# Stage transitions, LN3's residual and the mixer's constants placed elsewhere in a decoder layer on one core

## The chip, the cores and the metric

The kernel runs on one core of a Trainium2 chip. The core has a tensor engine (TensorE, PE in the profile; its weight loads are PEld), a vector engine (DVE), a scalar engine (ACT), GpSimd (POOL) and a sync engine (SP). They run their own instruction streams in order and wait for each other on semaphores. DMAs are issued from the queues of SP, ACT and POOL. The metric is the device time of one execution in microseconds (us); lower is better.

## The reference

One hybrid decoder layer on 256 tokens of width 2048, all in float32:

```
h = LN1(ALPHA*x + 0.5 * SwiGLU(x; ffn1))          # D_FF = 5632
m = mixer(h)      # latent attention (8 heads, RoPE) and differential attention (4 heads, ALiBi),
                  # both projected to 2048, gated by sigmoids, summed, times w_out
h = LN2(ALPHA*h + m)
out = LN3(ALPHA*h + 0.5 * SwiGLU(h; ffn2))

SwiGLU(x) = (silu(x @ w_gate) * (x @ w_up)) @ w_down
LN(x)     = (x - mean) * rsqrt(var + 1e-5) * g + b
```

ALPHA is 2 to the 1/4. The differential attention needs a causal mask with a slope times the distance of positions; RoPE needs sines and cosines of angles made from the positions; a scalar lambda is made from four small vectors.

## The kernel before

**Units.** Every product with a large weight matrix goes through one pipeline of *units* (`unit`, `advance`). A unit loads two 128-row blocks of weights, 512 columns wide (512 KB), splits them into a high part (cast to float32r on ACT, line 192) and a remainder (subtraction on DVE, line 193), and multiplies. Each product is the sum of three (high by high, low by high, high by low), so a unit has six 128x512 matmuls for each half `b` of the tokens (line 255). The split pairs live in a ring of `wring` tiles. Loads run a few units ahead, splits a few units ahead of the matmuls (`look(3, 4)` usually, `look(3, 2)` with the wide ring).

**Sevens.** Most matrix work is done in groups of seven products where eight would be needed: sums of weight blocks and of activations are formed first. Some of these sums are made by DVE (line 352), some by a DMA on POOL's queue that accumulates into a loaded block (line 357). Other units are *plain*: one load on SP's queue, one split, twelve matmuls. Results are read from PSUM with snapshots on ACT (line 428) and additions on DVE.

**Ticks.** The program's order is written by hand. `later(n, fn)` writes `fn` into the program n units on; `plan.at(i, fn)` attaches it to unit i; with `True` it is written when the unit is created. `tick()` ends every unit. Below this, the compiler's planner places each engine's instructions: by priority, which is the written order unless it is raised, among those that its own estimate of time says are ready. Once placed, each engine's order is fixed.

**Held-back halves.** Around a LayerNorm the second half of each unit (b=1) is held back: `widen()` sets `lag[0] = LAG` (seven units) and a ring of ten pairs, so that the b=0 products of the last units come first; `catch_up(n)` writes held halves until n remain. `one_lag` ends this.

**LayerNorm.** `LayerNorm.__init__` fetches the residual in four 128x1024 tiles `z` over POOL's queue and prepares it: for LN1 a multiplication by ALPHA on ACT; for LN2 and LN3, whose input `res` was stored before gain and shift were applied, a DVE multiplication and a DVE addition a tile with rows `gb` (line 523), themselves scaled by ALPHA on ACT (line 514). `evac` adds a finished PSUM bank to `z` (549 or 551) and takes statistics (553), all under a raised priority of 300 instructions. At the last chunk it calls `apply`, still under that priority: variance, square root, four normalised chunks (580), and at once the transposes `rows_to_quad` (458) with their copies into the next stage's activations, and a store of each chunk to `res`. LN3 has no transposes; its gain and shift rows come from `take_rows`, four loads at once, at the last eight units of the down pass.

**The feed-forward part** (`ffn`): gate/up units (opening of 16, then ten groups of 22), then the down pass in two column passes (`i` = 0 and 1) of sevens and plain (`lone`) units. The LayerNorm object is made at the first down unit.

**Around the mixer.** `setup` (mask on POOL, five small loads) is attached before the last eight units of FFN1's second down pass; `constants` follows 18 ticks later, that is in the mixer's opening: biases (769), angles and their range reduction (775 to 788), lambda (791 to 799). The opening ends with `kr_done`, whose transposes (816) feed the rotary key. `qr_finish` and the branch's `done1` transpose their rows two and four ticks after the last product.

Of the kernel before, what the change touches and what calls it, by code (L numbers as in the profile page):

```python
# [11 lines left out]
F32 = mybir.dt.float32  # L12
# [3 lines left out]
ALU = mybir.AluOpType  # L16
AX = mybir.AxisListType

P = 128
# [3 lines left out]
KD = D // P  # L23
# [9 lines left out]
LAG = 7  # L33
# [28 lines left out]
def layer_kernel(ctx: ExitStack, tc: tile.TileContext, a: dict, out: bass.AP):  # L62
# [15 lines left out]
    def act_tile(shape, dt=F32, name="act"):  # L78
        return apool.tile(shape, dt, tag="act", name=nm(name), bufs=SLOTS)
# [39 lines left out]
    class Acts:  # L119
        def __init__(self, name, kept=()):  # L120
            self.name = name
            self.kept = kept
            self.tiles = {}
            self.ready = set()
            self.raws = {}
            self.forms = {}
# [360 lines left out]
        V.scalar_tensor_tensor(out=f, in0=t, scalar=3.0, in1=y, op0=ALU.add, op1=ALU.mult)  # L487
        return f

    def broadcast_rows(src):  # L490
        r = []
        for h in range(2):
            t = act_tile([P, 1024], F32, "gb")
            nc.gpsimd.dma_start(t, src[0:1, h * 1024:(h + 1) * 1024].partition_broadcast(P))
            r.append(t)
        return r

    class LayerNorm:
        def __init__(self, scale, residual, last, each, x=None, cols=None, prior=None):
            self.scale = scale  # L500
            self.x = x
            self.cols = None
            if cols is not None:
                self.cols = [small.tile([P, KD], F32, tag="cols", name=nm("cols"), bufs=4) for _ in range(2)]
                for t, src in zip(self.cols, cols):
                    nc.gpsimd.dma_start(t, src)
            self.each = each
            self.z = [[None, None], [None, None]]
            rows = {}

            def row(i, h):
                t = rows[i, h] = act_tile([P, 1024], F32, "gb")
                nc.gpsimd.dma_start(t, prior[i][0:1, h * 1024:(h + 1) * 1024].partition_broadcast(P))
                later(6, lambda: S.mul(t, t, ALPHA))

            def fetch(b, h):
                t = self.z[b][h] = act_tile([P, 1024], F32, "z")
                nc.gpsimd.dma_start(t, residual[b, :, h * 1024:(h + 1) * 1024])
                if prior is None:
                    later(8, lambda: S.mul(t, t, ALPHA))  # L520
                else:
                    for i, op in ((0, ALU.mult), (1, ALU.add)):
                        later(7 + i, lambda i=i, op=op: V.tensor_tensor(out=t, in0=t, in1=rows[i, h], op=op))  # L523
            n = 0
            for h in range(2):
                jobs = [] if prior is None else [lambda i=i, h=h: row(i, h) for i in range(2)]
                for f in jobs + [lambda b=b, h=h: fetch(b, h) for b in range(2)]:
                    later(n, f)
                    n += 2
            self.rows = last  # L530
            self.gb = None
            self.stats = [small.tile([P, 4, 6], F32, tag="bn", name=nm("bn"), bufs=4) for _ in range(2)]

        def take_rows(self):
            if self.cols is None:
                self.gb = [broadcast_rows(r) for r in self.rows]

        def at(self, c, b):
            return self.z[b][c // 2][:, (c % 2) * 512:(c % 2) * 512 + 512]
# [5 lines left out]
        def evac(self, c, b, bank):  # L545
            z = self.at(c, b)
            with tc.high_priority(offset=PRIOR):
                if self.scale == 1.0:
                    V.tensor_tensor(out=z, in0=bank, in1=z, op=ALU.add)
                else:  # L550
                    V.scalar_tensor_tensor(out=z, in0=bank, scalar=self.scale, in1=z,
                                           op0=ALU.mult, op1=ALU.add)
                V.bn_stats(self.stats[b][:, c, :], z)  # L553
                if c == 2 and b == 0:
                    S.activation(sm(1, "sq"), self.stats[b][:, c, 0:1], AF.Sqrt, scale=0.0)
                if c == 3:
                    self.apply(b)

        def apply(self, b):
            mv = sm(2, "mv")  # L560
            V.bn_aggr(mv, self.stats[b].rearrange("p a s -> p (a s)"))
            zs = [self.at(c, b) for c in range(4)]

            if self.cols is None:
                gs, bs = ([self.gb[i][c // 2][:, (c % 2) * 512:(c % 2) * 512 + 512] for c in range(4)] for i in range(2))

                def center(c):
                    V.scalar_tensor_tensor(out=zs[c], in0=zs[c], scalar=mv[:, 0:1], in1=gs[c],  # L568
                                           op0=ALU.subtract, op1=ALU.mult)
                r = rstd(mv[:, 1:2], LN_EPS, 1, lambda: center(0))  # L570
                for c in range(4):
                    if c > 0:
                        center(c)
                    V.scalar_tensor_tensor(out=zs[c], in0=zs[c], scalar=r, in1=bs[c],
                                           op0=ALU.mult, op1=ALU.add)
                    self.each(b, c, zs[c])
                return
            r = rstd(mv[:, 1:2], LN_EPS, 1)
            for c in range(4):
                V.tensor_scalar(out=zs[c], in0=zs[c], scalar1=mv[:, 0:1], scalar2=r,  # L580
                                op0=ALU.subtract, op1=ALU.mult)
                rows_to_quad(zs[c], b, self.x, c, *self.cols)
                self.each(b, c, zs[c])

    def ffn(n, x, wgu, wdn, residual, rows, each, first=None, nxt=None, cols=None, prior=None):
        hb = {}
# [35 lines left out]
            (ahead_of if first is not None else at)(i + 10, f)  # L622
        if first is not None:
            first(at, ahead_of)
        at(16, one_lag)

        hx = [Acts("h") for _ in range(2)]
# [13 lines left out]
        for i, (c0, c1) in enumerate(((0, 1), (2, 3))):  # L641
# [62 lines left out]
                return [lambda k=k: step(k) for k in range(5)]  # L704

            if i == 0:
                at(len(items), lambda: st.update(ln=LayerNorm(0.5, residual, rows, each, nxt, cols, prior)), True)
            items += lone(4)
            items += seven(0, (5, 6), False)
            items += lone(7)  # L710
            if i == 0:
                items += seven(1, (8, 9), True)
                items += lone(10)
            else:
                items += seven(1, (8,), True)
                if n == 1:
                    at(len(items), setup)
                at(len(items), lambda: st["ln"].take_rows(), True)
                at(len(items), widen, True)
                for m in range(2):  # L720
                    for q in (9, 10):
                        items += lone(q, (m, m), True)
# [19 lines left out]
    def setup():  # L742
        GP.memset(mask, 0.0)
        for o in (0, 256):
            GP.affine_select(out=mask[:, o:o + P], in_=mask[:, o:o + P], pattern=[[-1, P]],
                             compare_op=ALU.is_ge, fill=NEG, base=0, channel_multiplier=1)
        pos_i = sm(2, "pos_i", I32)
        nc.gpsimd.dma_start(pos_i, a["pos_col"])
        row_i = tmp_tile([P, T], "row_i", I32)
        nc.gpsimd.dma_start(row_i, a["pos_row"].partition_broadcast(P))  # L750
        invf = tmp_tile([P, HALF], "invf")
        nc.gpsimd.dma_start(invf, a["inv_freq"].partition_broadcast(P))
        lv = tmp_tile([P, 4, P], "lv")
        nc.gpsimd.dma_start(lv.rearrange("p a n -> p (a n)"), a["lam"].partition_broadcast(P))
        nc.gpsimd.dma_start(subg, a["subln_g"].partition_broadcast(P))
        later(18, lambda: constants(pos_i, row_i, invf, lv))

    def constants(pos_i, row_i, invf, lv):
        pos = sm(2, "pos")
        V.tensor_copy(pos, pos_i)  # L760
        npos = sm(2, "npos")
# [6 lines left out]
        for h in range(DH):  # L768
            V.scalar_tensor_tensor(out=bias[h], in0=dist, scalar=-SLOPES[h], in1=mask,
                                   op0=ALU.mult, op1=ALU.add)  # L770

        ang = tmp_tile([P, 2, 2, HALF], "ang")
        for b in range(2):
            for j in range(2):
# [12 lines left out]
        V.tensor_scalar(out=ang, in0=ang, scalar1=PI_LO, scalar2=-PI_LO, op0=ALU.min, op1=ALU.max)  # L787
        S.activation(sincos, ang, AF.Sin)

        lp = tmp_tile([P, 2, P], "lp")  # L790
        V.tensor_tensor(out=lp, in0=lv[:, 0:2, :], in1=lv[:, 2:4, :], op=ALU.mult)
        ls = sm(2, "ls")
# [52 lines left out]
    def mixer(x, norm):  # L845
# [96 lines left out]
        def qr_finish(n, b, bank):  # L942
            t = tmp_tile([P, 512], "qr")
            tv = t.rearrange("p (h j i) -> p h j i", h=MH, j=2)
            rope(tv[:, :, 0, :], tv[:, :, 1, :], bank, b, MH)
            later(2, lambda: park_cols(t, qrp[b]))

        items += opening(x, [a[f"wc{n}"][0] for n in range(3)], c_done, (512, 288, 288))
        for i, f in enumerate(x.sevens(0)):
# [146 lines left out]
        def branch(f):  # L1096
# [5 lines left out]
            def done1(b, bank):  # L1102
                V.tensor_tensor(out=g1[:, b, :], in0=bank, in1=g1[:, b, :], op=ALU.mult)
                V.tensor_tensor(out=g0[:, b, :], in0=g0[:, b, :], in1=g1[:, b, :], op=ALU.add)
                later(4, lambda: rows_to_quad(g0[:, b, :], b, yq, f))

            def open_gates():
                for t in (g0, g1):
# [122 lines left out]
```

## Time and profile before

| | us |
|---|---|
| median of 3 runs | 2042.49 |
| lowest, highest | 2042.34, 2049.31 |
| the profiled execution | 2040.43 |
| its span, first to last instruction | 2038.4 |

The profile is of one execution. Its page gives busy time by engine, the span in slices, DMA queues and the costliest groups; further views answer for a stretch of time or a line: groups of instructions, an engine's timeline with the idle time before each piece and what ended it, waits between engines, and busy time and granted TensorE clock by window. Times in them are us from the start of the span. By the timeline FFN1's gate/up runs to about 452, its down pass to about 711, the mixer to about 1318 with w_out last, FFN2's gate/up to about 1775, and its down pass to 2027; LN3 ends the program.

### The profile page before, as it was taken

What the parts mean: (1) busy time and instruction counts of PE and PEld (TensorE: products, weight loads), DVE (VectorE), ACT (ScalarE), POOL (GpSimd) and SP (SyncE); (2) the same over time, 40 slices, a digit from 0 to 9 for tenths busy, and PEclk for the clock granted to TensorE, in tenths of its full rate; (3) what the DMA queues carried; (4) which work ended last, traced back from release to release, by engine and by line L of the source; (5) the groups of instructions that cost most, each with busy time, mean ns of one, the idle gap of its engine ahead of it and who ended that gap; (6) DMA issues with size and microseconds to landing.
All of it is one profiled execution on the core that took longest, in us unless ns stands there. A gap on an engine that the chain in (4) does not pass through costs nothing. (4 is left out here: it accounts for less than half of the span.)

```text
span 2038.4 us, 25557 instructions
## 1 busy us (share of the span) xinstructions
PE 1986.5 (97%) x8908; PEld 1636.8 (80%) x8908; DVE 1679.2 (82%) x1955; ACT 1250.0 (61%) x1587; POOL 280.0 (14%) x429
## 2 busy tenths in 40 slices
PE   9999999999999999999999999999999999989997
PEld 8888888877888778888878788778888888768885
DVE  7888888888989887588888675568888888899897
ACT  6666666666656686566667644466666666656563
POOL 1211121111000000211111100002111211110010
PEclk9999999999999999999999999999999999999999
DMA  9888888898879677898887955568888888898784
GB/s 317 232 252 250 247 231 251 245 289 272 277 254 271 201 222 247 227 287 249 263 254 229 340 198 192 173 232 247 249 245 240 242 244 252 280 296 274 249 265 157
DMA packets 160129, 506.64 MB, mean 249 GB/s; under 512 B 18992, under 2 KB 28288, under 8 KB 160000
## 3 DMA queue, kind: packets, MB, share of 16 engines
q1 hardware_dynamic: 99072, 352.89, 49.2%
q0 software_dynamic: 35104, 115.94, 25.9%
q10 hardware_dynamic: 25824, 36.18, 5.3%
q8 instruction: 69, 1.13, 0.2%
q14 instruction: 60, 0.49, 0.1%
HBM read 474.01 MB, written 30.93 MB: 248 GB/s over the span
## 5 line engine op out<-in xcount | busy, mean ns | idle before, releaser
L255 PE MATMUL mm<-wring,h 128*128 128x512 f32 (+1 forms) x3456 | 800.8, 386 | 11.3 <-DVE h L193 5.2
L255 PEld LDWEIGHTS mm<-wring,h 128*128 128x128 f32 x3456 | 635.5, 188 | 148.3 <-DVE h L193 8.4
L192 ACT CAST wring<-sraw 128x1024 fp32r<-128x1024 f32 x490 | 510.7, 1051 | 387.0 <-DVE sraw L352 123.5
L255 PE MATMUL mm<-wring,xs 128*128 128x512 f32 x2940 | 704.2, 391 | 5.9 <-ACT wring L192 4.4
L193 DVE TENSOR_TENSOR wring<-sraw,wring 128x1024 fp32r<-128x1024 f32 x490 | 592.5, 1218 | 121.0 <-ACT wring L192 113.7
L193 DVE TENSOR_TENSOR wring<-raw,wring 128x1024 fp32r<-128x1024 f32 (+1 forms) x462 | 548.9, 1204 | 166.9 <-ACT wring L192 165.2
L255 PEld LDWEIGHTS mm<-wring,xs 128*128 128x128 f32 x2940 | 551.4, 188 | 123.1 <-ACT wring L192 5.7
L192 ACT CAST wring<-raw 128x1024 fp32r<-128x1024 f32 (+1 forms) x462 | 471.2, 1040 | 284.9 <-PE mm L255 167.9
L255 PE MATMUL mm<-wring,x 128*128 128x512 f32 x1152 | 269.3, 390 | 1.9 <-ACT snap L428 1.8
L255 PEld LDWEIGHTS mm<-wring,x 128*128 128x128 f32 x1152 | 215.7, 188 | 48.6 <-ACT snap L428 2.8
L352 DVE TENSOR_TENSOR sraw<-sraw,sraw 128x1024 f32<-128x1024 f32 x140 | 168.6, 1218 | 0.3
L357 POOL DMA_DIRECT2D sraw<-in_gu_dram x80 | 69.4, 872 | 477.3 <-DMA raw<-in_gu_dram 295.4
L593 POOL DMA_DIRECT2D hT<-blocks x176 | 97.3, 562 | 205.9 <-DVE blocks L591 204.1
L255 PE MATMUL mm<-wring,y 128*128 128x512 f32 x384 | 89.1, 390 | 0.0
L255 PEld LDWEIGHTS mm<-wring,y 128*128 128x128 f32 x384 | 72.2, 188 | 14.9
L357 POOL DMA_DIRECT2D sraw<-in_dn_dram x32 | 27.3, 853 | 391.1 <-DVE wring L193 245.5
L428 ACT COPY snap<-mm 128x512 f32<-128x512 f32 x108 | 62.4, 578 | 5.0 <-PE mm L255 5.0
L612 DVE TENSOR_TENSOR gus<-mm,snap 128x512 f32<-128x512 f32 x80 | 54.8, 685 | 3.9 <-PE mm L255 3.9
L599 ACT ACTIVATE sg<-gus 128x256 f32<-128x256 f32 x80 | 33.2, 415 | 24.6 <-DVE gus L612 24.6
L255 PE MATMUL mm<-wring,om 128*128 128x512 f32 x192 | 46.0, 397 | 0.0
L255 PE MATMUL mm<-wring,od 128*128 128x512 f32 x192 | 44.2, 389 | 0.0
L255 PEld LDWEIGHTS mm<-wring,om 128*128 128x128 f32 x192 | 36.6, 192 | 7.6
(233 smaller groups left out, 1003.4 us busy)
## 6 DMA issues: line engine op xcount, KB each, us to landing
raw<-in_gu_dram SPq DMA_DIRECT2D x192, 512.0 KB, 4.7
sraw<-in_gu_dram SPq DMA_DIRECT2D x120, 512.0 KB, 6.9
raw<-in_dn_dram SPq DMA_DIRECT2D x112, 512.0 KB, 5.2
sraw<-in_gu_dram POOLq DMA_DIRECT2D x80, 512.0 KB, 8.0
sraw<-in_dn_dram SPq DMA_DIRECT2D x48, 512.0 KB, 6.9
hraw<-hT ACTq DMA_DIRECT2D x44, 512.0 KB, 5.0
sraw<-in_dn_dram POOLq DMA_DIRECT2D x32, 512.0 KB, 8.8
raw<-in_w_out_dram SPq DMA_DIRECT2D x32, 512.0 KB, 3.3
```

What stands on the lines that cost most here:

```text
L192: S.copy(hi, src)
L193: V.tensor_tensor(out=lo, in0=src, in1=hi.bitcast(F32), op=ALU.subtract)
L255: PE.matmul(o, x, w, start=first and i == 0, stop=last and i == len(whole) - 1, skip_group_check=True)
L352: V.tensor_tensor(out=t, in0=t, in1=self.blocks[joins[p], s], op=ALU.add)
L357: nc.gpsimd.dma_start(self.blocks[adds[p], s], self.w[1][4 * d + s], accum_op=ALU.add)
L428: S.copy(st["t"][i], bk[n])
L593: nc.gpsimd.dma_start(hT[q, b].rearrange("(g r) (i f) -> i r g f", g=4, i=4)[i], t[32 * i:32 * (i + 1), :].rearrange("r (g f) -> r g f", g=4))
L599: S.activation(sg, gate, AF.Silu)
L612: V.tensor_tensor(out=t, in0=bank, in1=snap, op=op)
```

## The change

1. `LayerNorm.apply` is divided. `normalise` (statistics, chunks, stores) keeps the raised priority. The transposes go to `turn`, outside it. For b=0 it writes four held halves, the transposes of chunk 0, one half, chunk 1, one half, chunk 2, one half, chunk 3, and sets the lag to zero, so that the last unit's b=1 half follows at once. For b=1 it writes chunk c's transposes 4 + c ticks later and sets the lag to seven again for the next stage.
2. For LN3 the residual's gain, shift and ALPHA are applied in FFN2's gate/up, from unit 46 on: `polish` fetches rows and tiles five ticks apart, multiplies, adds, and stores the result back to `res`. LN3's object then only fetches it, two ticks apart. LN2's fetches come three ticks apart instead of two.
3. LN3's gain and shift rows are loaded one a unit, attached to the last eight units' first four, instead of four at once when the first of them is created.
4. `setup` moves to the end of FFN1's first down pass, and `constants` is divided into masks, angles and lambdas, 6, 7 and 8 ticks after it, in plain units.
5. The transposes of `qr` come three ticks after their product instead of two, those of the branch's rows five instead of four.

```diff
+    def halves(residual, prior, gap, got, done=None, raw=False):
+        rows = {}
+        def row(i, h):
+            t = rows[i, h] = act_tile([P, 1024], F32, "gb")
+            nc.gpsimd.dma_start(t, prior[i][0:1, h * 1024:(h + 1) * 1024].partition_broadcast(P))
+            later(6, lambda: S.mul(t, t, ALPHA))
+        def fetch(b, h):
+            t = act_tile([P, 1024], F32, "z")
+            nc.gpsimd.dma_start(t, residual[b, :, h * 1024:(h + 1) * 1024])
+            got(b, h, t)
+            if raw:
+                later(8, lambda: S.mul(t, t, ALPHA))
+            if prior is None:
+                return
+            for i, op in ((0, ALU.mult), (1, ALU.add)):
+                later(7 + i, lambda i=i, op=op: V.tensor_tensor(out=t, in0=t, in1=rows[i, h], op=op))
+            if done is not None:
+                later(9, lambda: done(b, h, t))
+        n = 0
         for h in range(2):
...
+            for f in jobs + [lambda b=b, h=h: fetch(b, h) for b in range(2)]:
+                later(n, f)
+                n += gap
+    def polish(res, prior):
+        def back(b, h, t):
+            nc.gpsimd.dma_start(res[b, :, h * 1024:(h + 1) * 1024], t)
+        halves(res, prior, 5, lambda b, h, t: None, back)
...
+            halves(residual, prior, 2 if prior is None else 3, got, raw=raw)
...
-        def take_rows(self):
-            if self.cols is None:
-                self.gb = [broadcast_rows(r) for r in self.rows]
+        def take_row(self, i, h):
+            if self.gb is None:
+                self.gb = [[None, None], [None, None]]
+            t = self.gb[i][h] = act_tile([P, 1024], F32, "gb")
+            nc.gpsimd.dma_start(t, self.rows[i][0:1, h * 1024:(h + 1) * 1024].partition_broadcast(P))
...
                 if c == 3:
-                    self.apply(b)
-        def apply(self, b):
+                    self.normalise(b)
+            if c == 3 and self.cols is not None:
+                self.turn(b)
+        def normalise(self, b):
...
-                rows_to_quad(zs[c], b, self.x, c, *self.cols)
                 self.each(b, c, zs[c])
+        def turn(self, b):
+            def one(c):
+                rows_to_quad(self.at(c, b), b, self.x, c, *self.cols)
+            if b == 0:
+                for c in range(4):
+                    catch_up(3 - c)
+                    one(c)
+                lag[0] = 0
+            else:
+                for c in range(4):
+                    later(4 + c, lambda c=c: one(c))
+                lag[0] = LAG
...
+        if prior is not None:
+            at(KD + 30, lambda: polish(residual, prior))
...
-                at(len(items), lambda: st.update(ln=LayerNorm(0.5, residual, rows, each, nxt, cols, prior)), True)
+                at(len(items), lambda: st.update(ln=LayerNorm(0.5, residual, rows, each, nxt, cols, None, prior is None)), True)
...
                 items += seven(1, (8, 9), True)
+                if n == 1:
+                    at(len(items) - 4, setup)
                 items += lone(10)
             else:
                 items += seven(1, (8,), True)
-                if n == 1:
-                    at(len(items), setup)
-                at(len(items), lambda: st["ln"].take_rows(), True)
+                if rows is not None:
+                    for k in range(4):
+                        at(len(items) + k, lambda k=k: st["ln"].take_row(k % 2, k // 2))
                 at(len(items), widen, True)
...
-        later(18, lambda: constants(pos_i, row_i, invf, lv))
+        for k, part in enumerate(constants(pos_i, row_i, invf, lv)):
+            later(6 + k, part)
     def constants(pos_i, row_i, invf, lv):
+        return [lambda: masks(pos_i, row_i), lambda: angles(pos_i, invf), lambda: lambdas(lv)]
...
-            later(2, lambda: park_cols(t, qrp[b]))
+            later(3, lambda: park_cols(t, qrp[b]))
...
-                later(4, lambda: rows_to_quad(g0[:, b, :], b, yq, f))
+                later(5, lambda: rows_to_quad(g0[:, b, :], b, yq, f))
```

More of the change, by code (lines that the diff above doesn't have):

```diff
@@ L488, in rstd, with __init__ @@
         return f
-    def broadcast_rows(src):
-        r = []
-        for h in range(2):
[L493 to L496, printed above, removed]
+    def halves(residual, prior, gap, got, done=None, raw=False):
[17 more added lines that the diff above has]
+        n = 0
+        for h in range(2):
+            jobs = [] if prior is None else [lambda i=i, h=h: row(i, h) for i in range(2)]
+            for f in jobs + [lambda b=b, h=h: fetch(b, h) for b in range(2)]:
[5 more added lines that the diff above has]
+        halves(res, prior, 5, lambda b, h, t: None, back)
     class LayerNorm:
-        def __init__(self, scale, residual, last, each, x=None, cols=None, prior=None):
+        def __init__(self, scale, residual, last, each, x=None, cols=None, prior=None, raw=False):
             self.scale = scale
@@ L508, in __init__, with got @@
             self.z = [[None, None], [None, None]]
[L509 to L529, printed above, removed]
+            def got(b, h, t):
+                self.z[b][h] = t
+            halves(residual, prior, 2 if prior is None else 3, got, raw=raw)
             self.rows = last
@@ L755, in setup, with masks @@
         nc.gpsimd.dma_start(subg, a["subln_g"].partition_broadcast(P))
-        later(18, lambda: constants(pos_i, row_i, invf, lv))
+        for k, part in enumerate(constants(pos_i, row_i, invf, lv)):
+            later(6 + k, part)
     def constants(pos_i, row_i, invf, lv):
+        return [lambda: masks(pos_i, row_i), lambda: angles(pos_i, invf), lambda: lambdas(lv)]
+    def masks(pos_i, row_i):
         pos = sm(2, "pos")
@@ L770, in constants, with angles @@
                                    op0=ALU.mult, op1=ALU.add)
+    def angles(pos_i, invf):
+        pos = sm(2, "pos")
+        V.tensor_copy(pos, pos_i)
         ang = tmp_tile([P, 2, 2, HALF], "ang")
@@ L788, in constants, with lambdas @@
         S.activation(sincos, ang, AF.Sin)
+    def lambdas(lv):
         lp = tmp_tile([P, 2, P], "lp")
```

## The prediction

> **What bounds the kernel now.** The first part of the page shows TensorE busy nearly throughout, so I asked the windows view what an undisturbed stretch looks like.
>
> ```profile
> span 2038.4 us, 25557 instructions
> PE 1986.5 (97%) x8908; PEld 1636.8 (80%) x8908; DVE 1679.2 (82%) x1955; ACT 1250.0 (61%) x1587; POOL 280.0 (14%) x429
> 200.00:300.00 100.00, 100.00 (x443) 82.66 (x442) 85.26 (x89) 62.20 (x75) 17.47 (x26) 1.00 0.85 244
> ```
>
> The window row gives us, then busy time of PE, PEld, DVE, ACT and POOL, granted clock, DMA share and GB/s. 443 matmuls fill 100 us, so one takes 0.226 us, a half unit of six 1.36 us, a whole unit 2.71 us. No matmul is added or removed: the change can only win back the time in which TensorE stands still, and the half clock that follows. So I read the idle times in the PE timeline, stage by stage (in brackets: idle before, and what ended it).
>
> ```profile
> 692.72 1.94 PE L458 MATMUL tr<-ident,z 128*128 128x128 f32 x16 [1.81 <-DVE z L580]
> 694.41 16.62 PE L255 MATMUL mm<-wring,h 128*128 128x512 f32 x86
> 712.12 2.02 PE L458 MATMUL tr<-ident,z 128*128 128x128 f32 x16 [1.09 <-DVE z L580]
> 715.23 1.22 PE L255 MATMUL mm<-wring,h 128*128 128x512 f32 x3 [1.09 <-ACT h L192]
> 762.02 0.30 PE L816 MATMUL tr<-ident,kr_row 128*128 128x128 f32 x1 [2.90 <-DVE kr_row L811]
> 827.91 0.63 PE L888 MATMUL tr<-ident,qr 128*128 128x128 f32 x4 [1.35 <-DVE qr L811]
> 1167.45 0.66 PE L458 MATMUL tr<-ident,rows 128*128 128x128 f32 x4 [1.43 <-DVE rows L1104]
> 1169.78 1.12 PE L458 MATMUL tr<-ident,rows 128*128 128x128 f32 x4 [1.68 <-DVE rows L1104]
> 1312.41 3.45 PE L458 MATMUL tr<-ident,z 128*128 128x128 f32 x16 [4.60 <-DVE z L580]
> 1315.51 1.89 PE L255 MATMUL mm<-wring,y 128*128 128x512 f32 x6
> 1340.95 2.02 PE L458 MATMUL tr<-ident,z 128*128 128x128 f32 x16 [0.43 <-DVE z L580]
> 1344.06 2.15 PE L255 MATMUL mm<-wring,h 128*128 128x512 f32 x7 [1.09 <-ACT h L192]
> ```
>
> In each the tensor engine has reached a transpose whose rows DVE hasn't finished. In the LN2 transition (1312) old matmuls (y) still run after the transposes: work was there to cover the 4.60 us.
>
> **LayerNorm transposes and held-back halves.** The change puts four held halves, 24 matmuls, 5.4 us, between the last b=0 half and the first transpose, and a half ahead of each later chunk. LN2: 5.4 covers 4.60; the idle time goes. The sixteen transposes there took 3.45 instead of 1.94, at half clock:
>
> ```profile
> 1312.40:1315.90 3.50, 3.49 (x17) 3.50 (x18) 1.61 (x4) 2.53 (x7) 2.35 (x4) 0.53 0.56 199
> ```
>
> so 1.51 go with it. For b=1 the transposes come four ticks later, behind three units of the next stage, 18 matmuls as before: 0.43 stays. The next stage's b=1 halves now wait up to seven units, so the 1.09 for ACT's h goes. LN2: 4.60 + 1.51 + 1.09 = **7.2** (bounds: 1.1, the last part alone, and 7.6, with the 0.43). At LN1 much of the cover exists already:
>
> ```profile
> 688.36 0.68 DVE L551 SCALAR_TENSOR_TENSOR z<-mm,z 128x512 f32<-128x512 f32 x1
> 692.02 1.92 DVE L580 TENSOR_SCALAR z<-z,mv,f 128x512 f32<-128x512 f32 x4
> ```
>
> PE ran until 690.91, past the start of the b=0 evacuation at 688.36, so held halves already stood there. I take 0.5 of the 1.81, keep the first 1.09, drop the second: **1.6** (0 to 4.0). The transposes lose their priority, and with them the copies and splits behind them on ACT and DVE; the next stage's first unit comes four halves and three groups of transposes after the first, at least 5.4 us, against about 3.1 between transposes and h in the second pair of rows (712.12 to 715.23): hidden; uncovered it costs the 1.09 again.
>
> **Later transposes.** qr comes one whole unit later, 2.71 against 1.35: **1.35** (0 to 1.35). The branch's rows likewise: 1.43 + 1.68 = 3.11, less 2.71: **2.7** (0 to 3.11). For the last branch this leaves one unit less before w_out reads y: the copies need under the 2.71 that remain, so 0; if a ring cast gets ahead on ACT, 1.1. LN2's residual loads go out every third unit instead of every second, on POOL: this only thins a burst, I count 0.
>
> **Masks and angles.** They leave the mixer's opening, where kr waits:
>
> ```profile
> L785 DVE SCALAR_TENSOR_TENSOR ang<-turns,ang 128x128 f32<-128x128 f32 x12 | 3.4, 286 | 0.0
> L769 DVE SCALAR_TENSOR_TENSOR bias<-dist,mask 128x384 f32<-128x384 f32 x4 | 2.0, 551 | 0.0
> L472 ACT ACT_TABLE_LOAD x2 | 2.6, 1283 | 0.0
> L795 ACT ACT_TABLE_LOAD x1 | 1.3, 1283 | 0.0
> L788 ACT ACT_TABLE_LOAD x1 | 1.3, 1283 | 0.0
> 755.00:767.00 12.00, 8.95 (x37) 6.72 (x36) 9.18 (x19) 9.75 (x16) 0.00 (x0) 0.86 0.58 159
> 1160.00:1172.00 12.00, 8.89 (x39) 7.00 (x38) 9.86 (x12) 7.52 (x9) 0.00 (x0) 0.89 0.79 295
> ```
>
> With the other small operations they are some 9 us of DVE (5.4 in these two rows; the rest an estimate from that), and the square root then needs no table load of 1.28 in the opening, since neither sine nor exponential is called in between. Of 2.90 I take about half, **1.5** (0 to 2.9): the second kr row still waits on ACT copies that queue behind ring casts. The clock means of 0.86 and 0.89 over 12 us stand for 1.7 and 1.3 us at most; with shorter waits I take **1.0** of these (0 to 3.0).
>
> The Trainium skill, in "TensorE: Matmul & The Clock Gate", section "What's actually happening", has the clock halved after a whole idle window of about 3.4 us. The row speaks against it in that strict form: 2.90 us idle sufficed. By the rule the 1.0 would be nothing and the sum 1.0 less.
>
> In plain down units the 9 us land on a stretch whose DVE is full:
>
> ```profile
> 564.00:572.00 8.00, 8.00 (x37) 6.60 (x37) 7.35 (x9) 6.54 (x9) 0.00 (x0) 1.00 0.92 327
> 572.00:580.00 8.00, 8.00 (x37) 6.63 (x36) 8.00 (x14) 3.32 (x4) 0.00 (x0) 1.00 0.67 243
> 596.00:604.00 8.00, 8.00 (x37) 6.64 (x36) 4.70 (x5) 4.62 (x5) 0.00 (x0) 1.00 0.93 303
> ```
>
> Cover: four prepared units, up to 10.8 us where all are plain; the deficit is worked off after 596. Cost: **2** of 0 to 9, near the lower end because of the cover. The five small loads and POOL's mask are moved ahead of the second pass's accumulating DMAs on POOL; POOL is idle in the first two of these rows, so nothing. No load of SP's queue is moved.
>
> **LN3's residual.** FFN2's down pass loses eight DVE and four ACT operations and four row loads. Its twin in FFN1 never had the DVE part:
>
> ```profile
> 1774.00:1831.00 57.00, 47.96 (x206) 38.27 (x206) 51.55 (x57) 36.63 (x48) 10.04 (x16) 1.00 0.89 292
> 452.00:509.00 57.00, 54.99 (x239) 44.14 (x238) 50.67 (x58) 40.33 (x52) 7.90 (x12) 1.00 0.87 283
> L523 DVE TENSOR_TENSOR z<-z,gb 128x1024 f32<-128x1024 f32 x8 | 9.8, 1219 | 0.0
> L514 ACT ACTIVATE gb<-gb 128x1024 f32<-128x1024 f32 x4 | 4.2, 1059 | 4.2 <-DMA gb<-in_ln_g_dram 3.8 <-DMA gb<-in_ln_b_dram 0.4
> ```
>
> PE idles 9.04 of 57 us there and 2.01 in the twin. **7.0** (4 to 9: 9 is all of the idle time, 4 the ACT time that goes if DVE's share turns out to have been waiting time anyway; the twin, which I take, says what stays late, since it keeps all other work of the stage). In gate/up the same work returns, with four stores and a second set of loads, spread over 44 units:
>
> ```profile
> 1418.00:1500.00 82.00, 81.84 (x362) 67.44 (x360) 70.55 (x73) 50.88 (x61) 15.78 (x24) 1.00 0.84 244
> DVE z L523 <- DMA z<-res: 5.7, 1, 5.7
> z<-res POOLq DMA_DIRECT2D x8, 512.0 KB, 13.0
> sraw<-in_gu_dram POOLq DMA_DIRECT2D x80, 512.0 KB, 8.0
> GB/s 317 232 252 250 247 231 251 245 289 272 277 254 271 201 222 247 227 287 249 263 254 229 340 198 192 173 232 247 249 245 240 242 244 252 280 296 274 249 265 157
> ```
>
> DVE's free time, 11.45 of 82 us, holds the 9.8, leaving 1.7: nearly saturated, but four units of lead cover a burst. DMA carries 12 x 0.52 MB more, 77 GB/s beside 244; the 321 together are under the 340 that one slice of the page reaches, so I count no DMA bound. POOL's queue takes twelve issues; behind a store that waits for DVE stand the accumulating DMAs of the sevens, and behind these the casts on ACT that read them. ACT's four multiplications can hold up the snapshots behind them, as the 4.2 us of waiting for row loads above show for the down pass. Cost: **2** of 0 to 9.8, because the free time is there on paper and only its lumps are not.
>
> **End of the down pass.** LN3's gain and shift rows are loaded one a unit, no longer four at once:
>
> ```profile
> 1995.68 4.74 PE L255 MATMUL mm<-wring,xs 128*128 128x512 f32 x18 [1.51 <-ACT wring L192]
> 1983.71 10.08 DMA raw<-in_dn_dram
> ```
>
> A raw load took 10.08 us behind them. They are still 2 MB in the same stretch: **0.5** of 0 to 1.5; landing too late for LN3 would cost about 1.
>
> **Sum.** 7.2 + 1.6 + 1.35 + 2.7 + 1.5 + 1.0 + 7.0 + 0.5 = 22.85, less 4 = 18.85 us. The profiled execution took 2040.43 (span 2038.4), so 2021.6; against the median of 2042.49, which lies 2.1 higher, 2023.6. All gains at their upper and costs at their lower ends give 2009, all the other way 2058.
>
> **Rivals.**
> 1. *DVE becomes the bound* in gate/up and the plain units: both costs at their ends, 9.8 + 9 instead of 4, 14.8 more: 2038.4. For it: 8.00 of 8.00 at 572, 98% forecast at 1418. Against: PE never stopped at 572.
> 2. *The order on TensorE isn't the written one.* Instructions are placed by a planner's estimate; if it brings the transposes forward again, LN1 and LN2 keep their waits, 8.8 more: 2032.4. Against: the transposes lose the priority that had put them ahead of the y matmuls.
> 3. *Slower: POOL's queue in gate/up.* A store or load that waits in order holds the accumulating DMAs behind it, eight in 82 us, and a later seven needs each (landing 8.0 already). The one wait measured for such a residual is 5.7; eight times that is 45.6, less one cover of 7.4 (four units at 82/44 us): 38 lost, 2062. It decides from (18.85 + 7.4 + 10.2) / 8 = 4.6 us each. Against: the spacing of five units thins the burst in which 5.7 arose.
>
> **Chances.** 0.5% of the median, about what a measurement of this kernel can tell from no change, is 10.2 us: faster below 2032.3, slower above 2052.7. Forecast 0.62 (its own range 2011 to 2032), rival 1 0.16 (same), rival 2 0.13 (on the border, half and half), rival 3 0.09. Faster 0.69, same 0.22, slower 0.09. Range 2011 to 2038.5: it holds the forecast, rival 2 and most of rival 1.
>
> **What would show it.** Right: no idle time before the first LN2 transpose and no window below clock 1.0 there; four groups of transposes with matmuls between; the twin windows alike, near 2 us idle; kr's wait under 1.5. Wrong: idle PE between 1420 and 1500 with ACT or DVE waiting on sraw or z (rivals 1, 3); idle PE near 565 to 600; sixteen transposes still in one block after an idle time (rival 2).

## The result and the profile after

| us | before | after |
|---|---|---|
| median of 4 runs each | 2042.41 | 2024.91 |
| lowest, highest | 2040.99, 2049.31 | 2024.1, 2025.39 |
| the profiled execution | 2040.43 | 2025.39 |

The medians lie 17.5 us apart. The ratio, worked out from all the runs and not from the medians, is 0.9907, with a 95% interval of 0.9885 to 0.993, that is 14 to 23 us. The forecast was 2023.6.

The first lines of the page of after, to be held against those of before:

```profile
span 2022.6 us, 25562 instructions
PE 1982.5 (98%) x8908; PEld 1638.5 (81%) x8908; DVE 1678.5 (83%) x1956; ACT 1249.1 (62%) x1585; POOL 283.4 (14%) x437
```

The engines do the same work (DVE 1679.2 before, 1678.5 now); what shrank is the time in which TensorE stands. The PE timeline of after at the places that the prediction looked at (start, duration, what, count, and in brackets the idle time before and what ended it; line numbers of the new code are higher by some 35):

```profile
698.20 0.60 PE L458 MATMUL tr<-ident,z 128*128 128x128 f32 x4
698.55 1.64 PE L255 MATMUL mm<-wring,h 128*128 128x512 f32 x6
...
760.47 0.33 PE L851 MATMUL tr<-ident,kr_row 128*128 128x128 f32 x1 [0.62 <-DVE ms L895]
...
824.88 0.63 PE L923 MATMUL tr<-ident,qr 128*128 128x128 f32 x4 [0.32 <-ACT wring L192]
...
1164.49 1.03 PE L458 MATMUL tr<-ident,rows 128*128 128x128 f32 x8
...
1307.15 1.57 PE L458 MATMUL tr<-ident,z 128*128 128x128 f32 x12
1308.48 1.41 PE L255 MATMUL mm<-wring,y 128*128 128x512 f32 x5
1309.73 0.60 PE L458 MATMUL tr<-ident,z 128*128 128x128 f32 x4
...
1796.56 1.52 PE L255 MATMUL mm<-wring,xs 128*128 128x512 f32 x6
1800.67 2.92 PE L255 MATMUL mm<-wring,xs 128*128 128x512 f32 x6 [2.59 <-ACT wring L192]
...
1993.18 18.56 PE L255 MATMUL mm<-wring,h 128*128 128x512 f32 x74 [2.00 <-DVE wring L193]
```

The waits before the LayerNorm transposes are gone at LN1 (1.81 and 1.09 before) and LN2 (4.60). LN1's transposes stand in groups of four between halves of six matmuls, as written; at LN2 three groups are in one block, behind the held halves. kr, qr and the branch's rows wait 0.62, 0.32 and nothing (2.90, 1.35 and 3.11 before). The start of the last down pass keeps one wait of 2.59.

But there are new waits. The same view at two places where before had none to speak of:

```profile
596.12 0.73 PE L255 MATMUL mm<-wring,xs 128*128 128x512 f32 x2 [0.59 <-DVE wring L193]
...
597.73 0.49 PE L255 MATMUL mm<-wring,h 128*128 128x512 f32 x1 [0.64 <-ACT h L192]
600.89 2.50 PE L255 MATMUL mm<-wring,h 128*128 128x512 f32 x5 [2.67 <-DVE h L193]
...
1433.42 12.37 PE L255 MATMUL mm<-wring,h 128*128 128x512 f32 x42 [3.49 <-ACT snap L428]
...
1478.85 3.47 PE L255 MATMUL mm<-wring,h 128*128 128x512 f32 x14 [1.77 <-ACT snap L428]
```

Both are where the change put work: 600 is the plain units with masks and angles, 1430 and 1478 the gate/up units with LN3's residual. The windows view prices them (us given; busy time and count of PE, PEld, DVE, ACT and POOL; granted clock, DMA share, GB/s). Before:

```profile
590.00:608.00 18.00, 18.00 (x81) 14.68 (x80) 14.30 (x14) 9.50 (x11) 0.88 (x2) 1.00 0.87 254
1403.00:1440.00 37.00, 37.00 (x165) 30.66 (x164) 31.05 (x33) 22.54 (x28) 7.88 (x12) 1.00 0.86 242
```

After:

```profile
565.00:604.00 39.00, 35.09 (x146) 28.12 (x145) 39.00 (x73) 22.71 (x28) 1.68 (x2) 0.94 0.79 255
590.00:608.00 18.00, 14.09 (x50) 10.57 (x49) 16.72 (x31) 13.15 (x15) 1.68 (x2) 0.81 0.92 283
1403.00:1440.00 37.00, 33.51 (x137) 27.17 (x136) 31.82 (x31) 20.25 (x25) 10.09 (x17) 0.91 0.94 298
1418.00:1500.00 82.00, 76.75 (x326) 62.68 (x325) 70.92 (x74) 48.70 (x59) 19.23 (x31) 0.96 0.94 300
1774.00:1831.00 57.00, 54.41 (x233) 44.43 (x232) 49.64 (x56) 33.79 (x41) 7.86 (x12) 0.97 0.82 264
```

Counting matmuls tells the loss with the half clock in it: 50 instead of 81 between 590 and 608 are 31 x 0.226 = 7.0 us; 326 instead of 362 between 1418 and 1500 are 8.1 us. The clock columns, 0.81 and 0.91, say that the idle times at 600 and at 1430 were followed by a stretch at half speed; the 1.77 at 1478 wasn't (clock 1.00 from 1470 to 1482). And in the down-pass window 233 stand against 206: 27 x 0.226 = 6.1 us won.

**Why DVE is late at 600.** Its timeline in after:

```profile
597.38 0.28 DVE L819 SCALAR_TENSOR_TENSOR ang<-turns,ang 128x128 f32<-128x128 f32 x1
597.58 1.22 DVE L193 TENSOR_TENSOR wring<-raw,wring 128x1024 fp32r<-128x1024 f32 x1
598.72 0.28 DVE L819 SCALAR_TENSOR_TENSOR ang<-turns,ang 128x128 f32<-128x128 f32 x1
598.92 1.21 DVE L193 TENSOR_TENSOR wring<-sraw,wring 128x1024 fp32r<-128x1024 f32 x1
600.06 0.18 DVE L820 TENSOR_SCALAR ang<-ang 128x64 f32<-128x64 f32 x1
600.16 0.68 DVE L193 TENSOR_TENSOR h<-hraw,h 128x512 fp32r<-128x512 f32 x1
```

DVE had been busy for 39.00 of 39.00 us since 565. TensorE stood from 598.22 to 600.89 for the split of `h` at 600.16, which ran behind the angle steps and two weight splits: one engine, one order.

**Why PE stops at 1430.** POOL's timeline in after, and the landing time of the first of its two `z` loads, from the view of line 500 between 1411 and 1412.2:

```profile
1410.15 0.86 POOL L357 DMA_DIRECT2D sraw<-in_gu_dram  x1 [1.36 <-DVE sraw L352]
1410.72 0.85 POOL L495 DMA_DIRECT2D gb<-in_ln_g_dram  x1
1411.26 0.85 POOL L495 DMA_DIRECT2D gb<-in_ln_b_dram  x1
1411.80 1.36 POOL L500 DMA_DIRECT2D z<-res  x2
1430.45 0.54 POOL L519 DMA_DIRECT2D res<-z  x1 [17.30 <-DVE z L507]
```

```profile
DMA to landing us min/median/max: 12.5/12.5/12.5
```

Then DVE's and ACT's timelines and one piece of the chain of waits:

```profile
1424.39 1.23 DVE L507 TENSOR_TENSOR z<-z,gb 128x1024 f32<-128x1024 f32 x1 [3.31 <-ACT wring L192]
```

```profile
1430.90 1.04 ACT L192 CAST wring<-raw 128x1024 fp32r<-128x1024 f32 x1 [6.59 <-DMA raw<-in_gu_dram]
```

```profile
1421.11 9.71 DMA raw<-in_gu_dram
```

The first four loads of `polish` are written five units (some 9 us, at 44 units in 82 us) apart, but nothing holds them, and they are issued within 2 us of each other. The DMA line of the same 37 us and a little more (1400 to 1440, one figure a us) shows what follows:

```profile
GB/s 397 336 0 66 139 119 172 279 262 74 135 197 213 209 209 340 397 410 430 410 426 406 393 373 361 418 422 426 418 410 426 406 385 426 274 324 180 90 205 205
```

For some 18 us from 1416 the traffic stays near 410. The first `z`, issued at 1411.80, lands 12.5 later, at 1424.3, and that is when DVE goes on with the multiplication of it, after 3.31 us: the bracket names ACT, whose cast ended at the same moment, but the multiplication reads `z`. The chain to TensorE goes past this, by a weight load: it goes out at 1421.11, as a DVE split frees its buffer, and lands 9.71 later (its median over the program is 4.7); ACT waits 6.59 for it, in order, with the snapshot that frees a PSUM bank behind it, and PE waits for the snapshot. The shorter wait at 1478 stands at the end of a chain of the same kind, through a weight load of 7.99.

### The profile page after: what moved, and what is told of

It is laid out like the page before. It is cut to its first block, busy times and chain, and to the rows that moved or that the text cites. A ratio compares the mean times of both kernels' runs of the same rounds, so it can differ in the third digit from the quotient of the medians.

```text
span 2022.6 us, 25562 instructions
## 1 busy us (share of the span) xinstructions
PE 1982.5 (98%) x8908; PEld 1638.5 (81%) x8908; DVE 1678.5 (83%) x1956; ACT 1249.1 (62%) x1585; POOL 283.4 (14%) x437
```

## The experiments

Where single executions have to be compared stage by stage I put the k-th matmul of one kernel beside the k-th of the other. All traces hold 8908, and the stages' ends have the same numbers. The table gives, for the stretches that matter, the time of before and each kernel's difference from it, in us (from one profiled execution each):

```
matmuls                    0-  2500-  2800-  3368-  3516-  5100-  5700-  6300-  6700-  7800-  8700-
                         2500   2800   3368   3516   3800   5700   6100   6700   7800   8200   8907
what is there           (FFN1) plain    LN1     kr     qr   rows    LN2  gate/up  rest   down    end
before                  571.8   68.2  116.3   36.9   59.5  137.3   95.8   91.1  250.0  101.2   51.3
after                    +3.0   +7.0   -9.8   -4.0   -1.0   -4.9   -7.7   +7.9   -0.6   -5.4   -0.6
changed_again            +3.9   +7.0   -9.8   -3.5   -0.2   -4.0   -7.5  +10.5   +1.5   -6.3   -0.7
turns_alone              +4.0   +1.0   -3.0   -3.4   +0.1   -4.9   -7.4   -0.5   +0.2   -0.9   +1.8
residual_back            +6.7   +4.9   -9.8   -4.0   -0.4   -3.7   -7.2   -0.2   +0.3   -0.2   -0.1
constants_back           +3.4   +0.1   -3.4   -3.3   -0.6   -4.3   -7.5   +7.7   -0.5   -8.7   -0.2
ticks_back               -0.2   +6.7   -9.8   -3.8   +0.1   -0.5   -7.5   +6.7   +2.1   -7.4   -0.6
transposes_first         +2.1   +5.9   -6.4   -2.7   -1.4   -4.3   +0.6  +10.6   -0.2   -7.2   -0.7
only_transposes_raised   +2.6   +7.1   -9.4   -3.5   -1.6   -3.8   -7.5   +7.3   -0.6   -7.4   -0.3
turns_raised             +0.4   +7.4   -0.8   -3.6   -1.6   -2.9   +5.8   +6.9   +0.3   -7.3   -2.2
polish_gap20             +3.9   +7.4   -9.8   -3.0   +0.2   -4.8   -7.2   -0.5   +4.2   -4.9   -1.4
polish_sp                +2.0   +6.8   -9.8   -3.5   -1.2   -4.5   -7.6   +4.4   +1.4   -6.0   -1.3
constants_wide           +1.0   +1.1   -6.1   -3.6   -1.6   -4.9   -7.6   +5.2   -0.2   -6.5   -1.7
both_wide                +3.4    0.0   -5.4   -3.5   -0.8   -4.9   -7.6   -0.5   +3.6   -6.3   -0.7
```

The first column is a yardstick: all kernels but the last two have the same program there as before (but for the first of the masks at its very end, where they are moved), and it differs by -0.2 to +6.7. Single executions, and medians too, are therefore not told apart by 2 or 3 us; a stretch that differs the same way in every kernel with an edit, and in none without it, is.

The theories: **A**, the whole gain lies in the transitions (parts 1 and 5), and the two moves of work (parts 2 and 4) pay for themselves at best; **the forecast's**, that the moves give some 5 us of their own, the residual above all.

**Which part gives the gain.** `turns_alone` keeps parts 1 and 5 and undoes the others (the two lines of `setup` and `constants` as in the second diff below):

```diff
-        if prior is not None:
-            at(KD + 30, lambda: polish(residual, prior))
...
-                at(len(items), lambda: st.update(ln=LayerNorm(0.5, residual, rows, each, nxt, cols, None, prior is None)), True)
+                at(len(items), lambda: st.update(ln=LayerNorm(0.5, residual, rows, each, nxt, cols, prior, prior is None)), True)
...
-            halves(residual, prior, 2 if prior is None else 3, got, raw=raw)
+            halves(residual, prior, 2, got, raw=raw)
...
-                        at(len(items) + k, lambda k=k: st["ln"].take_row(k % 2, k // 2))
+                        at(len(items), lambda k=k: st["ln"].take_row(k // 2, k % 2), True)
```

> The LayerNorm transposes and the later ticks alone; LN3's residual, the mixer's constants and LN3's row loads as before the change. Theory A (all of the gain is in the transitions; the two moves cost about what they win): 2042.4 less about 18 (LN1 4, LN2 8, the branch's rows 5, qr 1), 2024, within 3 us of the changed kernel. Theory B (the forecast's terms: residual 7 less 2, constants 2.5 less 2, rows 0.5): 2042.4 less 13, 2030.

Measured: 2025.93, ratio 0.9924 (0.99 to 0.9948). The median is that of the whole change within 1 us. By time alone the 13 us of theory B aren't excluded, since the interval reaches from some 11 to 20 us; the table decides. In this kernel the stretches of the transitions (LN1, kr, qr, rows and LN2) gain 18.6, where the forecast's terms give them some 13, and neither the losses near 600 and 1430 nor the gain in the down pass are there. Theory A stands, the forecast's falls.

`residual_back` undoes the move in part 2 alone (the first two edits above; the spacing of three ticks stays).

> The changed kernel with LN3's residual made in FFN2's down pass again. Theory A: the idle time and half clock near 1430 and 1477 (about 8 us) go, and the down pass loses about 5 again: 2022, some 3 faster than the changed kernel. Theory B (forecast, 7 less 2): 2030, 5 slower.

Measured: 2026.14, ratio 0.9922 (0.9899 to 0.9944). In the table the 7.9 of gate/up go to -0.2, and the down pass loses its 5.4: from matmul 6300 to 8200 after stands at +1.9, this kernel at -0.1. The time lies between the two expectations, and its interval overlaps with that of after; by the table the move is worth nothing, or costs about 2.

`constants_back` undoes part 4 alone:

```diff
-                if n == 1:
-                    at(len(items) - 4, setup)
...
+                if n == 1:
+                    at(len(items), setup)
...
-        for k, part in enumerate(constants(pos_i, row_i, invf, lv)):
-            later(6 + k, part)
+        later(18, lambda: [f() for f in constants(pos_i, row_i, invf, lv)])
```

> The changed kernel with masks, angles and lambdas back in the mixer's opening. Theory A: the idle time near 597 (4 us, and as much half clock, 7 in all) goes, kr's wait and its half clock come back (about 5): within 2 us of the changed kernel, 2023 to 2026. Theory B (the plain units cost nearly nothing, kr's gain is real): 2028 or more.

Measured: 2023.88, ratio 0.9916 (0.9888 to 0.9943). The 7.0 in the plain units go, LN1 gives 3.4 instead of 9.8: from 2500 to 3516 -6.6 here, -6.8 in after. Worth nothing either. Two things in the row are new. kr keeps its gain of 3.3 although masks and angles are back in the opening. And LN1 is worse by 6.4; its timeline shows where the wait before the first transposes is again:

```profile
696.84 0.63 PE L458 MATMUL tr<-ident,z 128*128 128x128 f32 x4 [1.47 <-DVE z L591]
```

The stretch around it, matmuls 2950 to 3040, takes 23.0 us in before, 22.7 here and 18.9 in after. Ahead of it, over matmuls 2650 to 2800, DVE is full in this kernel and has time left in after (this kernel first):

```profile
610.50:644.50 34.00, 34.00 (x151) 28.15 (x150) 34.00 (x37) 25.49 (x30) 5.08 (x7) 1.00 0.93 296
617.00:651.00 34.00, 34.00 (x151) 28.16 (x151) 31.45 (x34) 23.68 (x28) 1.70 (x2) 1.00 0.94 305
```

So about 4 of the 7 us lost at 600 come back before LN1. At matmul 2900 DVE has finished 394 or 395 splits (line 193) in every kernel that stalls at 600, and 392 in every kernel that doesn't: it is further ahead there. That it caught up while TensorE stood is the likely reason, but isn't shown alone: the order of DVE's instructions between the two places differs between these two groups of kernels too, and no run parts the two.

**Why the transitions gain: priority or place.** The diff both drops the raised priority of the transposes and writes held halves ahead of them. `turns_raised` gives all of `turn` the raised priority again:

```diff
-                self.turn(b)
+                with tc.high_priority(offset=PRIOR):
+                    self.turn(b)
```

> The changed kernel, with the transposes and their copies under the raised priority again; the held halves still stand ahead of them in the written order. If the written order makes the gain: LN1 and LN2 show no idle time over 1 us, 2025 again. If the lost priority makes it: the planner puts the transposes ahead of held halves again and LN2 loses 4 to 7 us: 2030 or more.

Measured: 2047.6, ratio 1.0017 (0.9998 to 1.0035). The whole gain was gone, but this doesn't answer the question: the priority also covered the held halves. In the PE timeline of this kernel at LN2 all matmuls on `y` stand ahead of the transposes, none behind them as in before, and the wait is longer than in before:

```profile
1329.18 3.67 PE L458 MATMUL tr<-ident,z 128*128 128x128 f32 x16 [8.50 <-DVE ve L470]
```

So two more. `only_transposes_raised` raises the transposes and leaves the halves:

```diff
-                rows_to_quad(self.at(c, b), b, self.x, c, *self.cols)
+                with tc.high_priority(offset=PRIOR):
+                    rows_to_quad(self.at(c, b), b, self.x, c, *self.cols)
```

> The changed kernel with only the transposes and their copies under the raised priority; the held halves keep theirs (the run that raised both also pulled the halves ahead of the b=0 products). If the written order is overruled by the priority alone: the sixteen b=0 transposes stand in one block again, LN2 waits 4 to 5 us at half clock as before the change, LN1 about 2: 2024.9 plus 8 to 9, 2033. If the priority doesn't matter once the halves are written first: 2025.

Measured: 2026.62, ratio 0.9909 (0.9892 to 0.9925), the time of after. The sixteen stand in one block again, as the first expectation had it, but without a wait, since the held halves are through before them:

```profile
1308.05 2.02 PE L458 MATMUL tr<-ident,z 128*128 128x128 f32 x16
```

`transposes_first` has the low priority, but writes the transposes as before, ahead of the held halves:

```diff
-            if b == 0:
-                for c in range(4):
-                    catch_up(3 - c)
-                    one(c)
-                lag[0] = 0
-            else:
-                for c in range(4):
-                    later(4 + c, lambda c=c: one(c))
-                lag[0] = LAG
+            for c in range(4):
+                one(c)
```

> The changed kernel with the transposes at normal priority, but written right behind the normalising, ahead of the held halves, and the lag untouched. If the loss of priority alone gives the gain: 2025. If the halves must be written ahead: the planner, which takes DVE for done too early, places the block of sixteen early, LN2 idles 4 to 5 us: 2033.

Measured: 2036.16, ratio 0.9949 (0.993 to 0.9969). Its PE timeline at LN2:

```profile
1305.96 3.65 PE L458 MATMUL tr<-ident,z 128*128 128x128 f32 x16 [4.60 <-DVE z L591]
1309.26 2.23 PE L255 MATMUL mm<-wring,y 128*128 128x512 f32 x6
...
1338.17 7.14 PE L255 MATMUL mm<-wring,h 128*128 128x512 f32 x29 [1.09 <-ACT h L192]
```

The wait of before is back to the hundredth, 4.60, with the half clock (3.65 for sixteen) and the 1.09 behind b=1; the LN2 stretch stands at +0.6 instead of -7.7, LN1 at -6.4 instead of -9.8. Place makes the gain; the priority of the transposes, high or low, doesn't matter once the halves are written ahead and keep their own.

**The later ticks.** `ticks_back` writes qr and the branch's rows at two and four ticks again (`later(3` to `later(2`, `later(5` to `later(4`).

> The changed kernel with qr's transposes two and the branch's four ticks after their product again. Forecast's terms: the waits of 1.35 and 3.11 come back, 4 slower, 2029, with idle time at the first branch's rows. Rival (the branch's wait went because LN2's residual loads are spread over every third unit): no idle time over 1 us at the rows, 2026.

Measured (five rounds): 2029.69, ratio 0.9931 (0.9909 to 0.9952). Its PE timeline has the old waits again:

```profile
820.90 0.63 PE L923 MATMUL tr<-ident,qr 128*128 128x128 f32 x4 [1.47 <-DVE qr L846]
...
1159.67 0.66 PE L458 MATMUL tr<-ident,rows 128*128 128x128 f32 x4 [1.00 <-DVE rows L1139]
1162.00 1.12 PE L458 MATMUL tr<-ident,rows 128*128 128x128 f32 x4 [1.68 <-DVE rows L1139]
```

The rows' stretch goes from -4.9 to -0.5; qr's moves by less than executions differ. One tick at the branch's rows is worth about 4 us. The rival falls twice: in `turns_alone` LN2's loads are two ticks apart again, and the rows keep their -4.9.

**Can the loss of the residual's move be avoided?** `polish_gap20` writes its loads 20 units apart instead of five (`halves(res, prior, 20, ...)`).

> The changed kernel with LN3's residual made over the whole of gate/up, jobs 20 units apart instead of 5. If the stalls at 1430 and 1477 (some 8 us with the half clock) are the burst of loads and DVE's wait for them: they go, 2017. If the planner draws the loads together whatever the written spacing, since nothing holds them on POOL's queue: an idle time over 3 us stays near the first jobs, 2023 to 2025.

Measured: 2023.32, ratio 0.9892 (0.987 to 0.9914). The 7.9 of the stretch are gone (-0.5), 4.2 appear further on, so the stall went as the first expectation had it and the time is that of the second. The weight load from the chain parts two causes of the stall. It is the 128th such load (`raw<-in_gu_dram`) of the program. In after it goes out when TensorE stands at matmul 6380, and takes 9.71 to land; here it goes out at the same matmul and takes 4.8; in before it goes out later, at matmul 6393, and takes 3.4. So it wasn't issued late, it landed late, and with the loads spread it doesn't.

`polish_sp` keeps five units, but issues the loads on SP's queue instead of POOL's.

> The changed kernel, spacing 5, with the loads of LN3's residual on SP's queue, where they stand between weight loads that wait for ring buffers; the stores stay on POOL. If the burst on POOL's queue is the cause: the loads are spaced by the queue, 2018 or less. If the 6.3 MB in 80 us are too much wherever they are issued: idle time of 5 us or more stays between 1410 and 1500, 2023 to 2027.

Measured: 2026.68, ratio 0.9903 (0.988 to 0.9926). The stretch costs 4.4 instead of 7.9: the wait of 3.49 is one of 0.40, and four waits between 1410 and 1500 add up to 3.7. The time isn't told apart from that of after, and matches neither expectation with its sign: inconclusive for the time. On SP the loads keep their place behind weight loads, and the large wait goes with their bunching; the smaller ones stay.

**Masks and angles where DVE has room.** `constants_wide` takes them to the gate/up units of FFN1, from unit 60 on, in 17 steps four units apart instead of three lumps; in its core:

```diff
+        if n == 1:
+            at(60, setup)
...
-            later(6 + k, part)
+            later(10 + 4 * k, part)
...
+        r = [start] + [lambda h=h: slope(h) for h in range(DH)] + [angle]
+        for stage in range(2):
+            parts = _parts_of_2pi()[:7 - 2 * stage]
+            r.append(whole)
+            r += [lambda p=parts[i:i + 2]: reduce(p) for i in range(0, len(parts), 2)]
+        return r + [finish, lambdas]
```

> The changed kernel with masks, angles and lambdas in FFN1's gate/up, in 17 steps four units apart. If the 7 us near 597 are DVE's full stretch: they go and the mixer's opening stays as in the changed kernel: 2018. If the cost follows the work (DVE is 86% busy in gate/up too, and the tables of silu must be loaded again): idle time of 3 us or more between 170 and 290: 2022 or more.

Measured (five rounds): 2022.56, ratio 0.9893 (0.987 to 0.9916). That is the time of the second expectation without its sign: the first column, which holds gate/up, stands at +1.0. The window view at 600 in this kernel:

```profile
590.00:608.00 18.00, 17.32 (x76) 13.69 (x75) 14.03 (x14) 10.18 (x12) 0.85 (x1) 1.00 0.95 289
```

The loss at 600 is 1.1 instead of 7.0, but LN1 gives 6.1 instead of 9.8. Of the 5.9 won, 3.7 go where time had come back before LN1.

`both_wide` joins `constants_wide` and `polish_gap20`, and `changed_again` is after itself, in the same rounds.

> The two spread forms together: constants as in the run before, LN3's residual over the whole of FFN2's gate/up (20 units apart). If both losses were places and not work: 2024.9 less 7 less 6, 2012, ratio 0.985. If they come back elsewhere: 2020 or more.

> The changed kernel itself, on the same chip as the three others, to compare with: 2025, ratio 0.991.

Measured (five rounds): `both_wide` 2017.9, ratio 0.9875 (0.9854 to 0.9897), the lowest median of the study; `changed_again` 2024.85, ratio 0.9907 (0.9885 to 0.993). Against after that is 7 us in the same rounds. Its interval overlaps with those of the two kernels that it joins, so that it is faster than each of them isn't shown. I had expected 2012. Windows of `both_wide`:

```profile
565.00:604.00 39.00, 39.00 (x173) 32.06 (x172) 34.03 (x43) 20.22 (x24) 1.69 (x2) 1.00 0.82 270
1403.00:1440.00 37.00, 37.00 (x165) 30.64 (x164) 31.28 (x32) 23.06 (x28) 6.25 (x10) 1.00 0.96 287
```

Both stalls are gone; 173 and 165 matmuls stand there as in before. The 5.4 at LN1 instead of 9.8 and the 3.6 later in gate/up are what the expectation lacked.

## Why the prediction came true, and where it didn't

The number was right, 18.85 us forecast and 17.5 measured; not all of its steps were. That it came so close is in part luck: two costs were far too low, and gains that were as far too small made up for them. Two of the prediction's own signs of being wrong did show: TensorE idle between 1420 and 1500 with DVE waiting for `z`, and TensorE idle near 600. In the stretches that the change touches, after stands at 7.0 - 9.8 - 4.0 - 1.0 - 4.9 - 7.7 + 7.9 - 0.6 - 5.4 - 0.6 = -19.1; the drift of the first column takes part of that back.

- **LN2, 7.2:** right in size and mechanism. The stretch gains 7.2 to 7.7 in every kernel that writes the halves ahead and doesn't raise their priority, and stands at +0.6 where they aren't ahead. One sign came out otherwise: three of the four groups of transposes are one block.
- **LN1, 1.6 (0 to 4.0):** mis-sized. With masks and angles left where they were, this stretch gains 3.0 to 3.4, and 5.4 to 6.1 with them in gate/up. I kept the first 1.09 of b=1; it went too, as its transposes now stand behind matmuls that were held.
- **qr, 1.35:** between +0.2 and -1.6 with the later tick; too small to be told apart. **Branch rows, 2.7 and part of 1.0 for the clock:** 2.9 to 4.9; the wait and the half clock behind it went together.
- **kr, 1.5 for the constants' leaving, and the rest of the 1.0:** size 2.7 to 4.0, and the attribution failed. With the constants back and the new order the gain is 3.3, with the old order and the constants gone 2.7, with both 4.0. Either is enough for most of it: I added up edits that remove the same wait.
- **Masks and angles in plain units, cost 2 (0 to 9):** the step that failed is "four prepared units" as cover. DVE had been full from 565 on and the lead was used up: 7.0. What I didn't have at all is that some 4 of it come back before LN1.
- **LN3's residual in gate/up, cost 2 (0 to 9.8):** 6.7 to 10.6 with the loads as in after. Two steps failed. "Spread over 44 units" and the spacing of five units: the loads weren't issued as they were written. And "no DMA bound" from a mean of 321 GB/s: locally it was above 400 for some 18 us, and the weight load that mattered took 9.71, against 4.8 at the same place with the loads spread.
- **Start of the down pass, 7.0 (4 to 9):** 4.9 to 8.7, right. The end of the pass, 0.5, lies below what executions differ by.

So the two costs were about 11 us too low, and kr, the rows and LN1, with the 4 us that came back there, made up for it. Of the rivals, the first had the right size (14.9 us lost where it said 18.8) and the right mechanism at 600, where DVE is full; in gate/up DVE is busy for 70.92 of 82 us and isn't the bound, a weight load is; the second is what `transposes_first` shows, at 11.7 us for LN1 and LN2 where I had 8.8; of the third two stalls came, 3.49 and 1.77 us, not eight, and both by a weight load on SP's queue, not by an accumulating DMA held on POOL's. Added up from its own terms, the prediction's ends come to 2010 and 2056 where it has 2009 and 2058; nothing hangs on that.

The clock: three waits of 0.59, 0.64 and 2.67 us with little between them, and one of 3.49, were followed by half speed, 12.4 us for 42 matmuls that need 9.5; so was a single wait of 2.59 (2.92 us for six matmuls after it, 1.52 before). The Trainium skill, "TensorE: Matmul & The Clock Gate", section "What's actually happening", asks for a whole idle window of about 3.4 us; the 2.59 don't agree with that strict reading.

**What stays open:** whether DVE's catching up or its other order gave the 4 us back before LN1; and what the 4 us are that appear later in gate/up when the loads stand 20 units apart. In `polish_gap20` two waits of 1.02 and 1.03 for ACT's snapshot stand there, at 1685 and 1727, and their chains go back to weight loads of 7.84 and 9.54; what slowed these isn't shown.

## What to carry to other kernels

When an engine waits for a result although it has other work, look for what is written behind the wait and could stand ahead of it; moving held work there gained 8 us at one place where changing priorities gained nothing. Work moved off a waiting stage onto another is only won if the engine has room there for the lump, not on average: split it into small steps, far apart. Loads that hang on nothing can go out together whatever the written distance, so look at when they are issued. And gains that remove the same wait don't add up: a wait of before can be won only once.

## What I hadn't expected of the hardware

A wait of TensorE isn't always all lost: after 7.0 us at 600, about 4 came back at the end of the same pass (matmuls 2950 to 3040 in 18.9 instead of 22.7 us), where DVE, the engine that was behind, had got further ahead. Whether it did so by going on while TensorE stood isn't shown alone. And four loads of 512 KB issued together stood at the head of 18 us near 410 GB/s, in which a weight load took 9.71 to land against a median of 4.7, although the mean over 1418 to 1500 is only 300.
